# A decoder layer in split fp32: where the split weights lie in memory, relative to the operand they are multiplied with

## The chip, the cores and the metric

The kernel runs on one core of a Trainium2 chip. The metric is device time in microseconds. The kernel before was run three times: median 452.47 us, lowest 451.15, highest 453.2. A further execution was profiled and took 451.82 us.

The core's engines run side by side and are joined by semaphores: TensorE (matrix products; PE in the profile, with PEld for its weight loads), VectorE (DVE), ScalarE (ACT), GpSimd (POOL), and SyncE (SP), which issues most transfers.

## The reference

One layer with two token mixers over one input x of 512 tokens by 1024 channels, fp32 throughout:

```python
h = rms_norm(x, norm_w)
proj = h @ w_in                          # 1024 x 5912: q, k, v, z of mixer A; q, three k/v, gates, z of mixer B; gate_m
o_a = moba_mixer(q_a, k_a, v_a)          # block-sparse attention, 8 heads of 64
k_cmp = rms_norm(compress(kc)); v_cmp = compress(vc)
o_b = nsa_mixer(q_b, k_cmp, v_cmp, ...)  # compressed, selected and window branches
y_a = o_a * silu(z_a);  y_b = o_b * silu(z_b)
g_m = sigmoid(gate_m)                    # 2048 columns
merged = g_m[:, :1024] * (y_a @ w_branch_a) + g_m[:, 1024:] * (y_b @ w_branch_b)
out = x + merged @ w_out
```

With 512 tokens every block and every window is in reach, so both attentions are dense and causal here.

## The kernel before

**Split products.** TensorE multiplies in a reduced fp32 format (fp32r). To keep the precision, the kernel splits each operand into a high part (hi) and the rest (lo) and adds three products, hi·hi, lo·hi and hi·lo (`mm3`, line 374). So a product of one 128-row slice is three matmuls, each with its own load of 128 x 128 stationary weights, and with 256 or 512 columns of the other operand streamed through.

**Weights.** All weights come as tiles of 128 x 512 in one fixed order, the list `tiles`. A `Stream` object (`W`) loads each raw tile by a DMA from SyncE's queue into one of six raw buffers; ScalarE or GpSimd copies it into a hi tile (lines 351 and 355), VectorE or GpSimd subtracts to give the lo tile (line 360). The hi and lo tiles lie in eight pairs of fixed buffers, `whi0` to `whi7` and `wlo0` to `wlo7`, in turn; some tiles of the early projections lie in att buffers instead.

**att.** A pool of 45 buffers of 128 x 512 floats holds nearly everything else: split activations, heads, sums. A new tile takes a free buffer, and waits by semaphore for the last reader of what was there.

**Order.** The order of instructions on each engine is written by a planner that runs while the kernel is built: chains of operations with estimated costs, taken by due time, and four streams (attention, the gemms, the compression, the norm) that share TensorE. The number of buffers of PSUM and of some SBUF tags enters the planner; the att pool does not. Attention and the projections run till about 344 us, with the gate pairs of z and of mixer A mixed in.

**The stages that the change touches.**

- *Compression* (`compress_w`, products in `gemm_chan`, line 677): the projections kc and vc with the weights as stationary operand and 512 columns of the normalized input (`hh`, `hl`) streamed; tile `pgc` in the profile, kc from 51.15 us on, vc between 85 and 96 us. The z projections of mixer A use the same function and name later.
- *Mixer B's gate pairs* (`gate_pair(1, j)`, line 1418, j from 0 to 3): the gate matrix in a Strassen-like scheme of seven products of half size (product numbers 1 to 7), two gate blocks of 128 channels at a time. Each product is four slices of three matmuls, weights stationary, 256 columns streamed (`hh`, `hl` or sums `th`). Tile `pgw`; four pairs from 347.85 us on, with the branch products (`pbr`, 512 columns) between them.
- *The last stage* (`last`, line 1634): merged @ w_out in the same scheme, in the order of products 1, 2, 6, 5, 7, 3, 4. Here the merged activations (`m`, `mh`, `ml`) are stationary and the weights W are streamed, 512 columns for each of two blocks of 128 tokens; of product 4, the second block is done in two halves of 256 columns. Tile `po`, 180 matmuls from 408 us on, then the residual is added on VectorE and stored.

**Where the tiles lie.** A hi or lo buffer is 512 + 32 floats wide, 2176 bytes, which is 8.5 times 256 bytes. hi and lo buffers alternate, so each lo buffer begins 128 bytes off the hi buffer's place modulo 256. `part` (line 604) chooses where in its buffer a tile starts: a tile with a shift begins 16 floats (64 bytes) in, and a lo tile without one begins 32 floats (128 bytes) in, its `side`. `att` buffers (2048 bytes), the input `hh`/`hl` (rows of 2048 bytes) and the other operands all lie at the same remainder modulo 256 as the hi buffers. In this text the distance of a product is the start of its W tile less that of the other operand, modulo 256 bytes: 0 for hi and lo without a shift; 64 (hi) and 192 (lo) with one. With a shift are the tiles under 512 wide (kb, vb) and all gate pairs; without one are kc, vc, the z of mixer A, the branch products and the last stage.

Of the kernel before, what the change touches and what calls it, by code (L numbers as in the profile page):

```python
# [13 lines left out]
F32R = mybir.dt.float32r  # L14
# [7 lines left out]
P = 128  # L22
# [12 lines left out]
POFF = [0, 128, 384, 768]  # L35
WT = 512
SHIFT = 16
NW = 8
AHEAD = 6
SLACK = 3e3  # L40
# [8 lines left out]
XSTEP = 3e3  # L49
XA = 0  # L50
LEAD = 17e3
RAWS = (6, 45)
NRAW, NATT = RAWS
LAND = 1000
SLOW = dict(D=1.01, A=1.01, P=1.05)
# [31 lines left out]
def chan_pieces():  # L87

    out = {"kc": KC, "vc": VC}
    for j in range(4):  # L90
        out[f"za{j}"] = ZA + 128 * j
    return out
# [13 lines left out]
def hybrid_kernel(ctx: ExitStack, tc: tile.TileContext, x, x0, xT, wtok, wchan, wz, wgate, gains, w1,  # L106
                  relone, wbr, wout, consts, out):
    nc = tc.nc
    cp = ctx.enter_context(tc.tile_pool(name="cp", bufs=1))
    wp = ctx.enter_context(tc.tile_pool(name="wp", bufs=NW))  # L110
    pg = ctx.enter_context(tc.tile_pool(name="pg", bufs=2, space=bass.MemoryType.PSUM))
# [9 lines left out]
    def nm(s):  # L121
        uid[0] += 1
        return f"{s}{uid[0]}"
# [304 lines left out]
    def att(name, dt=F32R):  # L428
        return ap_.tile([P, 512], dt, name=nm(name), tag="a")
# [111 lines left out]
    cnames = list(chan_pieces())  # L541

    def tok_tiles(name):
        i0, nt, n, kk = tlay[name]
        return [(wtok[i0 + i][:, :kk * n], kk * n) + (SHIFT,) * (n < WT) for i in range(nt)]

    def chan_tiles(name):
        return [(wchan[cnames.index(name), i], 512) for i in range(2)]

    ORDER_T = ("v", "qk0", "kc", "qk1", "vc", "kb", "qb", "vb", "za0", "za1", "za2", "za3")  # L550
    tiles = []
    for n_ in ORDER_T:
        tiles += tok_tiles(n_) if n_ in tlay else chan_tiles(n_)
    wsum = {w: drp.tile([4, n_, P, 512], F32, name=nm("wsum")) for w, n_ in (("z", 2), (0, 4), (1, 4), (2, 4))}

    def quads(w):

        return wz if w == "z" else wgate[w] if w < 2 else wout

    def operand(p_, w, j):  # L560

        s_ = wsum[w]
        return {1: lambda: quads(w)[0, j], 2: lambda: quads(w)[1, j], 4: lambda: quads(w)[3, j], 5: lambda: s_[0, j], 6: lambda: s_[1, j],
                3: lambda: s_[2, j], 7: lambda: s_[3, j]}[p_]()
# [18 lines left out]
    for q in SEQ:  # L583
        if q in range(8):
            tiles.append((wbr[q, 0], 512))
        else:
            tiles += [(operand(p_, "z" if q[0] == "z" else 0, int(q[1])), 512, SHIFT) for p_ in (1, 2, 6, 5, 7, 3, 4)]
    for j in range(4):
        for p_ in (1, 2):
            tiles.append((operand(p_, 1, j), 512, SHIFT))  # L590
        for p_ in (5, 6, 3, 7):
            tiles.append((operand(p_, 1, j), 512, SHIFT))
        tiles += [(wbr[j, 1], 512), (operand(4, 1, j), 512, SHIFT), (wbr[j + 4, 1], 512)]
    for p_ in (1, 2, 6, 5, 7, 3, 4):
        tiles += [(operand(p_, 2, k), 512) for k in range(4)]
    from_att = set()
    for n_ in ORDER_T:
        if n_ in tlay and tlay[n_][1] == KT:
            o_ = sum(len(tok_tiles(z)) if z in tlay else 2 for z in ORDER_T[:ORDER_T.index(n_)])
            from_att |= set(range(o_, o_ + KT, 2))  # L600
    shift = {i: SHIFT for i in range(len(tiles)) if tiles[i][2:]}
    tiles = [z[:2] for z in tiles]

    def part(name, tag, side):

        place = itertools.count()

        def f(i):
            z = shift.get(i, 0)
            if i in from_att:  # L610
                return att(name)[:, z:]
            b = next(place) % NW
            t = wp.tile([P, WT + 2 * SHIFT], F32R, name=nm(name), tag=f"{tag}{b}", bufs=1)
            return t[:, z or side:]
        return f
    W = Stream(tiles, NRAW - 1, part("wh", "whi", 0), part("wl", "wlo", 2 * SHIFT))
    W1 = W1_[0] = Stream([(w1[kv, q], 512) for kv in range(2) for q in range(8)], 1, lambda i: att("vh"), lambda i: att("vl"))

    def ahead(f):

        W.split(W.i + min(4, int(f * 4 + 0.8)))

    def gemm_tok(name, emit, tags="gggg"):
        _, nt, n, kk = tlay[name]
        ws = []
        for t in range(NT):
            yield room(tags[t])
            ps = psum(tags[t], "pgt")
            for k in range(KT):
                if not t and not k % kk:  # L630
                    ws += W.take(1, n)
                    W.split(W.i + min(nt - 1 - k // kk, 3))
                h = hh[:, k, t * P:(t + 1) * P], hl[:, k, t * P:(t + 1) * P], None
# [8 lines left out]
    def more(n, used):  # L642

        i = W.i
        while i < W.i + n:
            used += i not in from_att
            if used > NW:
                break
            i += 1
        W.split(i)  # L650

# [982 lines left out]
    def last(ms, xr):  # L1634
# [33 lines left out]
        for p_, z_, first in ((1, "a", True), (2, "c", True), (6, "a", False), (5, "b", True), (7, "a", False), (3, "b", False)):  # L1668
            for k in range(4):
                if p_ == 2:  # L1670
                    xr[k, 1] = att("xr", F32)
                    dma(xr[k, 1], x[k * P:(k + 1) * P, 512:], 2048)
                w = W.take(1, 512)[0]
                for t in range(2):
                    if not k:
                        if first:
                            yield room(tags[z_][t])
                            ps[z_, t] = psum(tags[z_][t], "po")
                        else:
                            yield rd[z_, t].ready  # L1680
                    yield from part(ps[z_, t], p_, t, k, w, full, first, not first)
                    if k == 3:
                        rd[z_, t] = add(z_, t, *out_of(p_, t), full)
                        if (p_, t) == (7, 1):
                            add(z_, t, t, 1, False, False, H[1])
        ws = W.take(4, 512)
        for t, z_, z in ((0, "a", full), (1, "a", H[0]), (1, "d", H[1])):
            if z_ == "d":
                yield room("g")
                ps[z_, t] = psum("g", "po")  # L1690
            else:
                yield rd[z_, t].ready
            for k in range(4):
                yield from part(ps[z_, t], 4, t, k, ws[k], z, z_ == "d", z_ == "a")
            add(z_, t, *out_of(4, t), z)
# [122 lines left out]
```

## Time and profile before

| what | us |
|---|---|
| median of 3 runs (lowest, highest) | 452.47 (451.15, 453.2) |
| the profiled execution | 451.82 |
| its span | 450.0 |
| TensorE busy | 442.1 (98%) |
| VectorE busy | 382.5 (85%) |
| ScalarE busy | 302.6 (67%) |
| GpSimd busy | 202.6 (45%) |

A row of a group names line, engine, operation, output<-inputs (of a matmul: the streamed operand, then the stationary one), shape and count. In the chain and in the list of instructions the first two columns are the start and the length in us. A matmul's length runs from its start to the end of its results, and the next one starts long before that; the time that a matmul costs is the distance between two starts. A row of a stretch gives the stretch, the sum, then for each engine its busy time and the number of its instructions that touch the stretch, then the granted clock, the DMA share and GB/s.

### The profile page before, as it was taken

Reading aid. Unit: us, or ns where it says so; the run is one execution under the profiler, and the core shown is the slowest. Engines: PE = TensorE matmul, PEld = TensorE weight load, DVE = VectorE, ACT = ScalarE, POOL = GpSimd, SP = SyncE. Lnnn points to the kernel's source line nnn. Section 1 sums busy time; section 2 is a strip of 40 time slices with the busy share of each in tenths; the row PEclk is TensorE's granted clock in tenths of the full one; section 3 lists DMA queues with packets and bytes.
Section 4 is the critical chain, followed back from the end, with each engine's and each line's share of the span. In section 5 each row is a group of like instructions: output and inputs, shape, how many; then the busy total and the mean of one; then the engine's idle time right before and its main releaser. Section 6 shows DMA issues by size and latency. Waiting matters only on the chain.

```text
span 450.0 us, 8536 instructions
## 1 busy us (share of the span) xinstructions
PE 442.1 (98%) x2779; PEld 394.4 (88%) x2779; DVE 382.5 (85%) x938; ACT 302.6 (67%) x710; POOL 202.6 (45%) x239
## 2 busy tenths in 40 slices
PE   8999999999999999999999999999999999999996
PEld 7888888899778899888999999989988999998885
DVE  5998899889998796879899899977967698899783
ACT  6875778867978798376878777687764355455450
POOL 1364337866675573077675654664850222211000
PEclk9999999999999999999999999999999999999999
DMA  8886646887965869958977876986767888899862
GB/s 263 279 278 212 216 150 207 179 248 182 269 175 168 213 213 282 294 142 189 291 215 212 212 187 175 250 223 156 211 165 171 263 219 253 219 246 313 275 219 95
DMA packets 54221, 98.21 MB, mean 218 GB/s; under 512 B 5216, under 2 KB 8160, under 8 KB 54176
## 3 DMA queue, kind: packets, MB, share of 16 engines
q1 hardware_dynamic: 38944, 68.30, 47.0%
q0 software_dynamic: 7616, 14.68, 20.2%
q10 hardware_dynamic: 7616, 14.68, 9.6%
q8 instruction: 22, 0.36, 0.3%
q14 instruction: 23, 0.19, 0.1%
HBM read 90.69 MB, written 36.31 MB: 282 GB/s over the span
## 4 chain that ended last, share of the span: by engine, by line
PE 82%; DVE 10%; ACT 3%; DMA 2%; issue 2%; SPq 0%; POOL 0%; ACTq 0%; DVEq 0%
PE pgw L385 19%; PE pgt L385 14%; PE pbr L385 10%; PE po L385 9%; PE pgc L385 7%; PE O L1097 6%; PE pt L1063 5%; PE pgf L667 4%; PE sps L1016 3%; PE sps L1017 3%; DMA wr<-in_w 1%; DVE wl L360 1%; DVE sb L1035 1%; DMA wr<-in_wtok 1%; DVE pl L1077 1%
## 5 line engine op out<-in xcount | busy, mean ns | idle before, releaser
L360 DVE TENSOR_TENSOR wl<-wr,wh 128x512 fp32r<-128x512 f32 (+1 forms) x150 | 102.9, 701 | 3.9 <-ACT wh L351 3.6
L351 ACT CAST wh<-wr 128x512 fp32r<-128x512 f32 (+1 forms) x130 | 76.9, 608 | 14.5 <-DMA wr<-wsum 6.1
L355 POOL TENSOR_SCALAR wh<-wr 128x512 fp32r<-128x512 f32 (+1 forms) x39 | 31.0, 807 | 77.7 <-DVE wl L360 21.1
L1054 POOL TENSOR_SCALAR P<-P,sst,gate 128x512 f32<-128x512 f32 (+3 forms) x56 | 46.2, 828 | 39.9 <-DVE sst L1053 31.8
L1050 ACT ACTIVATE P<-sb,sst 128x512 f32<-128x512 f32 (+3 forms) x88 | 50.8, 577 | 17.4 <-DVE sst L1035 15.7
L1035 DVE CUSTOM_DVE_ANT_0 sb<-sps,T 128x512 f32<-128x512 f32 (+3 forms) x96 | 45.9, 482 | 14.0 <-PE sps L1017 13.4
L385 PE MATMUL pgt<-wl,hh 128*128 128x512 f32 (+2 forms) x160 | 55.9, 349 | 0.8 <-DVE wl L360 0.8
L385 PE MATMUL pgt<-wh,hh 128*128 128x512 f32 (+2 forms) x160 | 56.6, 354 | 0.0
L385 PE MATMUL pgt<-wh,hl 128*128 128x512 f32 (+2 forms) x160 | 55.8, 348 | 0.0
L385 PE MATMUL pgw<-th,wh 128*128 128x256 f32 x240 | 48.9, 280 | 0.2 <-DVE gm L1508 0.2
L1075 ACT CAST ph<-pt 128x512 fp32r<-128x512 f32 (+2 forms) x72 | 33.8, 476 | 19.7 <-PE pt L1063 18.2
L385 PE MATMUL pgw<-hh,wh 128*128 128x256 f32 x160 | 45.1, 282 | 0.2 <-ACT c L1449 0.2
L385 PE MATMUL pgw<-hh,wl 128*128 128x256 f32 x160 | 44.4, 277 | 0.0
L385 PE MATMUL pgw<-hl,wh 128*128 128x256 f32 x160 | 44.4, 277 | 0.0
L1063 PE MATMUL pt<-cst,P 128*128 128x128 f32 x232 | 40.7, 273 | 0.4 <-DVE pl L1077 0.3
L1077 DVE TENSOR_TENSOR pl<-pt,ph 128x512 fp32r<-128x512 f32 (+2 forms) x72 | 38.7, 548 | 2.0 <-ACT ph L1075 1.7
L385 PEld LDWEIGHTS pgw<-th,wh 128*128 128x128 f32 x240 | 39.4, 188 | 0.7 <-DVE gm L1508 0.4
L426 POOL TENSOR_TENSOR nr<-nss,mhalf 128x8 f32<-128x8 f32 (+1 forms) x16 | 26.9, 1684 | 20.5 <-DVE nss L425 17.3
L385 PEld LDWEIGHTS pgt<-wl,hh 128*128 128x128 f32 x160 | 30.1, 188 | 5.1 <-DVE wl L360 1.2
L385 PE MATMUL pgw<-th,wl 128*128 128x256 f32 x120 | 33.3, 277 | 0.0
L385 PEld LDWEIGHTS pgt<-wh,hh 128*128 128x128 f32 x160 | 30.1, 188 | 3.4 <-ACT nraw L710 0.2
L385 PEld LDWEIGHTS pgt<-wh,hl 128*128 128x128 f32 x160 | 30.1, 188 | 3.2
(268 smaller groups left out, 1290.7 us busy)
## 6 DMA issues: line engine op xcount, KB each, us to landing
wr<-wsum SPq DMA_DIRECT2D x56, 256.0 KB, 4.3
wr<-in_wtok SPq DMA_DIRECT2D x36, 256.0 KB, 4.8
wsum<-in_wgate ACTq DMA_DIRECT2D x16, 512.0 KB, 5.0
wsum<-wsum POOLq DMA_DIRECT2D x14, 512.0 KB, 8.1
wr<-in_wgate SPq DMA_DIRECT2D x24, 256.0 KB, 5.2
xsum<-th SPq DMA_DIRECT2D x16, 256.0 KB, 2.1
T<-rtab SPq DMA_DIRECT2D x16, 256.0 KB, 5.3
wr<-in_w SPq DMA_DIRECT2D x16, 256.0 KB, 4.6
```

Source lines behind the costliest of these rows:

```text
L351: e.copy(hi, raw)
L355: e.tensor_scalar(hi, raw, 1.0, 1.0, op0=ALU.mult, op1=ALU.mult)
L360: c.do({"D": cd(n)} if lead else either(n), lambda e, hi=hi, lo=lo, raw=raw: e.tensor_sub(lo, raw, hi.bitcast(F32))).mark((w, 1, i))
L385: nc.tensor.matmul(dst, sts[i][a], mvs[i][b], start=(start and i == a == b == 0), stop=(stop and i == n - 1 and b == 1), skip_group_check= ...
L426: c.do({"p": 430 + POWC * w}, lambda e: e.tensor_tensor(v(dst), v(ss), mhalf[:parts, :w], op=ALU.pow))
L1035: e.tensor_tensor_reduce(z["sb"][:, :L], sps[:, :L], T[:, S - L:], scale=-1.0, scalar=3e38, op0=ALU.add, op1=ALU.min, accum_out=st[:, 0, b ...
L1050: e.activation(pv(), z["sb"][:, :L], AF.Exp, bias=st[:, 0, b:b + 1], scale=-1.0, accum_out=st[:, 1, b:b + 1])
L1054: c.do({"P": 315 + 0.834 * L}, lambda e: e.tensor_scalar(pv(), pv(), st[:, 2, b:b + 1], g, op0=ALU.mult, op1=ALU.mult))
L1063: nc.tensor.transpose(pt[:, (b - kb) * P:(b - kb + 1) * P], u.p0 if u.p0 is not None and b == 0 else u.pb[:, POFF[b] + kb * P:POFF[b] + (k ...
L1075: e.copy(z["w"][0], pt[:, :w])
L1077: ch.do({"D": cd(w)}, lambda e: e.tensor_sub(z["w"][1], pt[:, :w], z["w"][0].bitcast(F32)), pt)
L1097: nc.tensor.matmul(O[0][:, S - n:], v.bitcast(F32) if kb == 3 else v, w, start=(u.first and kb == 0 and i == 0), stop=(u.last and kb == 3 ...
```

## The change

Each product gets a shift of its own, in floats, and hi and lo tile get the same. A buffer becomes 512 + 64 floats wide, 2304 bytes or nine times 256, so that hi and lo buffers all begin at the same remainder and `side` goes. The 16 buffers grow by 128 bytes each; the att pool gives up one buffer of 2048 bytes for it.

In bytes, the distances become: last stage, products 1, 2, 6, 5, 7, 3, 4: 16, 32, 48, 64, 96, 240, 224 (all were 0). Mixer B's gate pairs 0 to 3: 32, 16, 96, 240 (were 64 and 192). kc 16, vc 240 (were 0). The other tiles with a shift keep 64 for hi and get 64 for lo in place of 192. The tiles without one keep 0.

```diff
 SHIFT = 16
+SHIFTS = {1: 4, 2: 8, 6: 12, 5: 16, 7: 24, 3: 60, 4: 56, "kc": 4, "vc": 60}
+SHIFT1 = (8, 4, 24, 60)
...
-RAWS = (6, 45)
+RAWS = (6, 44)
...
-        return [(wchan[cnames.index(name), i], 512) for i in range(2)]
+        return [(wchan[cnames.index(name), i], 512, SHIFTS.get(name, 0)) for i in range(2)]
...
         for p_ in (1, 2):
-            tiles.append((operand(p_, 1, j), 512, SHIFT))
+            tiles.append((operand(p_, 1, j), 512, SHIFT1[j]))
         for p_ in (5, 6, 3, 7):
-            tiles.append((operand(p_, 1, j), 512, SHIFT))
-        tiles += [(wbr[j, 1], 512), (operand(4, 1, j), 512, SHIFT), (wbr[j + 4, 1], 512)]
+            tiles.append((operand(p_, 1, j), 512, SHIFT1[j]))
+        tiles += [(wbr[j, 1], 512), (operand(4, 1, j), 512, SHIFT1[j]), (wbr[j + 4, 1], 512)]
     for p_ in (1, 2, 6, 5, 7, 3, 4):
-        tiles += [(operand(p_, 2, k), 512) for k in range(4)]
+        tiles += [(operand(p_, 2, k), 512, SHIFTS[p_]) for k in range(4)]
...
-    shift = {i: SHIFT for i in range(len(tiles)) if tiles[i][2:]}
+    shift = {i: tiles[i][2] for i in range(len(tiles)) if tiles[i][2:]}
...
-    def part(name, tag, side):
+    def part(name, tag):
...
-            t = wp.tile([P, WT + 2 * SHIFT], F32R, name=nm(name), tag=f"{tag}{b}", bufs=1)
-            return t[:, z or side:]
+            t = wp.tile([P, WT + 4 * SHIFT], F32R, name=nm(name), tag=f"{tag}{b}", bufs=1)
+            return t[:, z:]
         return f
-    W = Stream(tiles, NRAW - 1, part("wh", "whi", 0), part("wl", "wlo", 2 * SHIFT))
+    W = Stream(tiles, NRAW - 1, part("wh", "whi"), part("wl", "wlo"))
```

## The prediction, made before the changed kernel was timed

> **What bounds the kernel now.** I read the page's head and its chain first, then the chain in order of time for the last 110 us, then single instructions of TensorE in the three places that the change touches.
>
> ```profile
> span 450.0 us, 8536 instructions
> PE 442.1 (98%) x2779; PEld 394.4 (88%) x2779; DVE 382.5 (85%) x938; ACT 302.6 (67%) x710; POOL 202.6 (45%) x239
> ...
> PE 82%; DVE 10%; ACT 3%; DMA 2%; issue 2%; SPq 0%; POOL 0%; ACTq 0%; DVEq 0%
> ```
>
> TensorE sets the end: 98% busy and 82% of the chain. In the changed stages it is all of the chain (columns: start, length, what, how many):
>
> ```profile
> 348.01 8.17 PE pgw L385 x72
> 356.18 2.74 PE pbr L385 x12
> 358.92 1.37 PE pgw L385 x12
> ...
> 393.09 8.22 PE pgw L385 x72
> ...
> 404.05 1.37 PE pgw L385 x12
> 405.42 2.74 PE pbr L385 x12
> 408.16 38.40 PE po L385 x180
> 446.56 0.02 issue
> 446.59 0.42 DVE xr L1653
> ```
>
> Mixer B's four gate pairs are four groups of 72 and four of 12, 336 matmuls; the last stage is 180. A nanosecond on each of these is a nanosecond on the end. The length that counts is from one start to the next, not the mean of one instruction, since they overlap. So, single instructions (start, length), three in the gate pairs, then the last stage:
>
> ```profile
> 349.21 0.28 PE L385 MATMUL pgw<-hh,wh 128*128 128x256 f32 x1
> ...
> 350.57 0.28 PE L385 MATMUL pgw<-hh,wh 128*128 128x256 f32 x1
> ...
> 351.93 0.28 PE L385 MATMUL pgw<-th,wh 128*128 128x256 f32 x1
> ```
>
> There are 12 matmuls between each two of these rows: 1.36 us / 12 = 113.3 ns for 256 columns, with the weights 64 bytes (hi) and 192 bytes (lo) past the other operand, counted modulo 256.
>
> ```profile
> 411.40 0.39 PE L385 MATMUL po<-wh,mh 128*128 128x512 f32 x1
> ...
> 412.08 0.39 PE L385 MATMUL po<-wh,mh 128*128 128x512 f32 x1
> 412.31 0.39 PE L385 MATMUL po<-wh,ml 128*128 128x512 f32 x1
> 412.53 0.39 PE L385 MATMUL po<-wl,mh 128*128 128x512 f32 x1
> 412.76 0.39 PE L385 MATMUL po<-wh,mh 128*128 128x512 f32 x1
> ...
> 443.87 0.28 PE L385 MATMUL po<-wh,mh 128*128 128x256 f32 x1
> 443.99 0.28 PE L385 MATMUL po<-wh,ml 128*128 128x256 f32 x1
> 444.11 0.28 PE L385 MATMUL po<-wl,mh 128*128 128x256 f32 x1
> 444.23 0.28 PE L385 MATMUL po<-wh,mh 128*128 128x256 f32 x1
> ```
>
> With distance 0 the 512-column matmuls take 0.68 / 3 = 226.7 ns, and the 256-column ones of product 4 take 120 ns, 6.7 ns more than in the gate pairs. That is the one place where this trace shows a distance to matter. TensorE's weight loads show which limit it is:
>
> ```profile
> 443.52:444.95 1.43, 1.43 (x12) 1.00 0.18 66
> 347.85:349.21 1.36, 1.36 (x12) 1.00 0.69 164
> 408.68:415.47 6.79, 6.79 (x31) 5.63 (x30) 6.79 (x14) 3.25 (x7) 1.93 (x2) 1.00 1.05 365
> ```
>
> The first two rows are stretches seen by the weight loads alone: 12 loads in 1.43 us at distance 0, 12 in 1.36 us in a gate pair, back to back in both, so a slower load shows at once. In the third row, of 512-column work (columns: stretch, sum, PE, weight loads, then the other engines), loads fill only 5.63 of 6.79 us: a load that gets some nanoseconds slower or faster there is hidden by the streaming of 512 columns. And 226.7 is exactly twice 113.3: streaming costs 0.4427 ns per column in both, with distance 0 in the one and 64/192 in the other. I take that rate as a floor that the distance does not touch. The clock column is 1.00, so the clock is no part of it.
>
> **The change part by part.** It adds and removes no instruction, and the order is the same: the planner's costs are untouched, and it does not count the att tiles. What moves is addresses, and one att buffer goes.
>
> *Last stage, 156 matmuls of 512 columns* (products 1, 2, 6, 5, 7, 3 with 24 each, and 12 of product 4). Distance goes from 0 to 16, 32, 48, 64, 96, 240 and 224 bytes. By the floor above: 0. Bounds: no row has such a distance. Below, the best that a row has shown a distance to do is 6.7 ns a matmul, −1.04 us; above, distance 0 is already the slow row among those seen, so I bound it by the same step the other way, +1.04. I take 0, because loads have 1.16 us of slack in the 6.79 us row.
>
> *Last stage, 24 matmuls of 256 columns* (product 4, distance 0 to 224, that is 32 bytes to the other side). Ends 113.3 and 120 ns: −0.16 to 0. Half way between 0 and 64, I take half: −0.08 us.
>
> *Gate pairs, 4 × 84 matmuls of 256 columns.* Distance goes from 64/192 to 32, 16, 96, 240 for pairs 0 to 3. They stand on the floor now and have no slack in the loads, so there is more to lose than to win. Upper end, all as at distance 0: 336 × 6.7 = +2.24 us. Lower end, a load alone:
>
> ```profile
> 158.36 0.60 PE L1063 MATMUL pt<-cst,P 128*128 128x128 f32 x4
> ...
> L1063 PE MATMUL pt<-cst,P 128*128 128x128 f32 x232 | 40.7, 273 | 0.4 <-DVE pl L1077 0.3
> ```
>
> Four transposes span 0.60 us and the last lasts 0.273, so they start (0.60 − 0.273) / 3 = 109 ns apart; with only 128 columns to stream, that is the load's own pace. 336 × (113.3 − 109) = −1.44 us if floor and collision both went. I go by the nearest rows, in a straight line from 120 ns at 0 to 113.3 at 64 bytes on either side: 16 bytes (pairs 1 and 3) costs 5 ns, 32 bytes (pair 0) 3.3 ns, 96 bytes (pair 2) nothing. 84 × (3.3 + 5 + 0 + 5) = +1.12 us.
>
> A rule speaks against any of this. The Trainium skill, "TensorE: Matmul & The Clock Gate", section "Step-by-step: what each phase is for", gives TensorE two independent read ports, one for the moving operand and one for weight loads. By it the two could not collide, distance would be nothing and the whole sum 0; the 120 against 113.3 ns above does not agree with it, and I go with the rows.
>
> *Compression, 48 matmuls of 512 columns* (kc to 16 bytes, vc to 240).
>
> ```profile
> 51.15:56.59 5.44, 5.44 (x24) 4.32 (x23) 0.00 (x0) 1.00 0.69 230
> 85.44:95.59 10.15, 6.37 (x24) 4.17 (x24) 0.00 (x0) 1.00 0.84 189
> ...
> 93.38 5.96 DMA wr<-in_w
> ```
>
> kc is 24 matmuls in 5.44 us, 226.7 ns each, on the floor with loads at 4.32 of 5.44: 0, bounds ±0.16 by 6.7 ns each. vc is spread over 10.15 us among attention's work, and a weight transfer stands on the chain behind it (the chain's row at 93.38): 0, hidden by that transfer; ±0.16 if that cover went.
>
> *The lo tiles of the other shifted products* move from 192 to 64 bytes, where the hi tiles already are. Here, in the vb projection, W is the moving operand:
>
> ```profile
> 173.13 0.28 PE L385 MATMUL pgt<-wl,hh 128*128 128x256 f32 x1
> ...
> 174.31 0.28 PE L385 MATMUL pgt<-wh,hh 128*128 128x256 f32 x1
> ```
>
> Ten matmuls in 1.18 us, 118 ns; at worst 120, so 96 × 2 and the same for kb: 0 to +0.4 us; I take +0.1. The six gate pairs of z and mixer A have 168 lo matmuls (a third of 504), bounded by 6.7 ns each, 0 to +1.1; I take 0, as twice as many hi loads at 64 bytes go along with 113.3 ns.
>
> *44 att buffers instead of 45.* A writer of an att tile can wait for a reader that ends later. The densest place I found is VectorE's pair of y tiles ahead of the branch products:
>
> ```profile
> 312.49 0.68 DVE L1126 TENSOR_TENSOR ys<-O,ot 64x512 f32<-64x512 f32 x1
> 313.20 1.49 DVE L1145 TENSOR_TENSOR yl<-ys,yh 128x512 fp32r<-128x512 f32 x2
> 314.61 0.15 DVE L1053 RECIPROCAL sst<-sst 128x1 f32<-128x1 f32 x1
> ```
>
> A wait there holds up what is queued behind it on VectorE: the reciprocal of attention's softmax, which GpSimd and then TensorE's transposes need, and the next read of a score bank. Ends 0 and 1.49 us (the pair's own length again); I take +0.1, as TensorE has matmuls of other streams (branch products, gate pairs) queued between attention's and fills in with them; without that cover it is the 1.49.
>
> *The splits that write the tiles* write at another start, with the same count and shape; 0, hidden behind TensorE, whose gate pairs need nothing from VectorE on the chain.
>
> Sum: 0 − 0.08 + 1.12 + 0 + 0.1 + 0 + 0.1 = +1.24 us. The profiled execution took 451.82 us (450.0 of span and 1.8 around it), which gives 453.1. The runs' median is 452.47, 0.65 above that execution, inside a spread of 451.15 to 453.2; the straight line that carries the +1.12 is the weakest step, so I do not add the whole 0.65 on top: **453.0 us**.
>
> **The rivals.**
>
> *A, the distance frees the 512s too* (faster). The rate of 0.4427 ns a column would then be a collision that all distances in multiples of 64 bytes share. For it: every such distance in the trace is a multiple of 64 bytes. Against it: the cost grows with the columns streamed, not with the loads. Priced by the lower ends: −1.04 − 0.16 − 1.44 − 0.16 = −2.8 us, 449.0. A sentence beside it: the same page of the Trainium skill, section "Back-to-back issue gap", gives columns / 2.4 + 2.5 ns, an estimate of 215.8 ns for 512 and 109.2 for 256; by that all three stages would lose 156 × 10.9 + 24 × 10.8 + 336 × 4.1 + 24 × 10.9 = 3.6 us, 448.2. The rows here, 226.7 and 113.3, do not show it.
>
> *B, near distances collide harder* (slower). One mechanism, in the gate pairs: the load that runs beside 256 columns meets them in the same place of memory, and a distance of one or two 16-byte steps keeps the two together longer than distance 0. It is slower by over 0.5% once the four pairs average over 120 ns, where +2.24 is reached; at twice distance 0's loss, 126.7 ns, it is +4.5, 456.3. For it: loads have no slack there, 1.36 of 1.36 us. Against it: no row is above 120 in a quiet stretch.
>
> *C, the distance does nothing,* and 120 against 113.3 comes from which operand is the weights: product 4 loads m and streams W, the gate pairs the other way round. For it: the vb projection, W streamed too, takes 118 ns at 64 and 192 bytes. Then the sum is +0.2, 452.0 to 452.7.
>
> *D, the att buffer* bites: 1.49 us at its place and as much at one more, +3 us, 454.8. For it: VectorE's next attention step stands right behind the pair in the rows at 313 us, so nothing of a wait there is private. Against it: VectorE is 85% busy, not 98%, and can catch up. It decides from about 2.3 us of waits that reach TensorE.
>
> **How the numbers follow.** Forecast (between −1 and +2.2 us, 451.2 to 454.5) 0.55, C 0.20, A 0.11, B 0.09, D 0.05. About 0.5%, 2.3 us, is what a measurement of this kernel can tell from no change. Faster is A without its weak half and a little of the forecast's low side: 0.11. Slower is B, most of D and the top of the forecast: 0.14. The rest, 0.75, is within. The range takes half of A and of B: 450.0 to 455.2.
>
> **What would show it.** In the gate pairs, 12 matmuls should take 1.42 us in pairs 1 and 3 (118.3 ns each), 1.40 in pair 0 (116.6), 1.36 in pair 2. In the last stage 512 columns stay at 226.7 in every product, and product 4's halves fall to about 117 ns; 113.3 would mean that 32 bytes do as much as 64. If any product of the last stage is under 224 ns, A is right and the floor was none. If all gate pairs keep 1.36 us and the halves 120, C is right. If the gate pairs pass 1.44 us, B. A wait on an att tile would show as an idle stretch of VectorE around 313 us, with one of TensorE behind it. The forecast is wrong if the gate pairs together change by over 2.3 us.

## The result

The change makes the kernel slower: 455.42 us, median of 7 runs (454.43 to 456.03), against 452.31 us for 7 runs of the kernel before beside it. The ratio is 1.0071, with a 95% interval of 1.0056 to 1.0086: +3.2 us (2.5 to 3.9). The forecast was 453.0 us and "within 0.5%"; its range ended at 455.2. The profiled execution took 455.2 us, of which 453.4 are span, 3.4 more than before.

### The profile page after: what moved, and what is told of

It is laid out like the page before. It is cut to its first block, busy times and chain, and to the rows that moved or that the text cites. A ratio compares the mean times of both kernels' runs of the same rounds, so it can differ in the third digit from the quotient of the medians.

```text
span 453.4 us, 8542 instructions
## 1 busy us (share of the span) xinstructions
PE 444.6 (98%) x2779; PEld 396.2 (87%) x2779; DVE 382.6 (84%) x938; ACT 302.7 (67%) x710; POOL 201.6 (44%) x239
## 4 chain that ended last, share of the span: by engine, by line
PE 82%; DVE 11%; ACT 3%; issue 2%; DMA 2%; SPq 0%; DVEq 0%; ACTq 0%
PE pgw L387 18%; PE pgt L387 14%; PE pbr L387 9%; PE po L387 9%; PE pgc L387 7%; PE O L1099 6%; PE pgf L669 5%; PE pt L1065 5%; PE sps L1018 3%; PE sps L1019 3%; DVE wl L362 2%; DMA wr<-in_wbr 1%; DVE sb L1037 1%; DVE pl L1079 1%; DVE vl L362 1%
## 5 line engine op out<-in xcount | busy, mean ns | idle before, releaser
L1065 PEld LDWEIGHTS pt<-cst,P 128*128 128x128 f32 x232 | 29.1, 140 | 5.3 <-issue 1.5
```

The lines of the kernel that those rows point to most:

```text
L1065: nc.tensor.transpose(pt[:, (b - kb) * P:(b - kb + 1) * P], u.p0 if u.p0 is not None and b == 0 else u.pb[:, POFF[b] + kb * P:POFF[b] + (k ...
```

## The profile after

The head of the page and the engines' shares of the chain:

```profile
span 453.4 us, 8542 instructions
PE 444.6 (98%) x2779; PEld 396.2 (87%) x2779; DVE 382.6 (84%) x938; ACT 302.7 (67%) x710; POOL 201.6 (44%) x239
...
PE 82%; DVE 11%; ACT 3%; issue 2%; DMA 2%; SPq 0%; DVEq 0%; ACTq 0%
```

TensorE executes the same 2779 matmuls in the same order and is busy 2.5 us longer. The page counts 8542 instructions, 6 more than before; the difference is in semaphore instructions alone, and the kernel that changes nothing but the att buffers has it too. The chain in order of time from the gate pairs on (start, length, what, how many; helper lines are two further down than before):

```profile
348.82 8.52 PE pgw L387 x72
357.34 2.78 PE pbr L387 x12
360.12 1.42 PE pgw L387 x12
...
379.75 8.45 PE pgw L387 x72
388.20 2.74 PE pbr L387 x12
...
393.89 6.01 DMA wr<-in_wbr
...
400.07 0.40 ACT mh L1360
400.47 0.28 ACT c L1451
...
400.88 3.05 PE pgw L387 x24
403.94 2.76 PE pbr L387 x12
406.70 1.41 PE pgw L387 x12
...
410.86 39.07 PE po L387 x180
```

Against the rows of before, the 3.4 us fall into three stretches. The gate pairs begin at 348.82 in place of 348.01: +0.81. They and the branch products up to the last stage take 410.86 − 348.82 = 62.04 us in place of 408.16 − 348.01 = 60.15: +1.89. The last stage takes 39.07 in place of 38.40: +0.67. In the middle stretch, 72 gate matmuls take 8.52 (pairs 0 and 1) and 8.45 (pair 2) in place of 8.17, and 12 take 1.42 or 1.41 in place of 1.37; counted from start to start over all 336, the gate products account for +1.45. Most of the rest, about 0.4, is a stall in pair 3: its 72 matmuls take 8.87 us from start to start, and not 8.45 as in pair 2, because two groups of twelve took 1.76 and 1.49 us. There TensorE waited for ScalarE's c, which on the chain stands behind a transfer of branch weights.

The first stretch holds a wait of VectorE that before did not have (columns: start, length, instruction, and in brackets the idle time ahead of it and what ended that):

```profile
312.28 0.68 DVE L1128 TENSOR_TENSOR ys<-O,ot 64x512 f32<-64x512 f32 x1
314.09 1.49 DVE L1147 TENSOR_TENSOR yl<-ys,yh 128x512 fp32r<-128x512 f32 x2 [1.13 <-PE sps L1019]
315.50 0.15 DVE L1055 RECIPROCAL sst<-sst 128x1 f32<-128x1 f32 x1
```

It is the y pair that the prediction named. The row puts its wait down to a matmul of the scores, which has to read what lay in the att tile, and the reciprocal behind it goes from 314.61 to 315.50. TensorE then waits behind VectorE, which is late with its split of attention's transposed tile (first the row of before, then that of after; columns: who waited for whom, us in total, times, the longest):

```profile
PE pt L1063 <- DVE pl L1077: 0.3, 1, 0.3
PE pt L1065 <- DVE pl L1079: 1.4, 1, 1.4
```

The execution had been 0.21 us ahead of that of before at 311 us, so that stretch's +0.81 is +1.03 from there on, less 0.21.

## The experiments

**44 att buffers alone** (kernel before):

```diff
-RAWS = (6, 45)
+RAWS = (6, 44)
```

> The kernel before with 44 att buffers in place of 45 and nothing else; all distances stay. Theory T (the trace of after shows VectorE's yl pair 1.1 us late at 314 us, behind a matmul of the scores): the missing buffer alone costs 1.0 to 1.2 us, so the time is 1.1 us above before (ratio 1.0025), the pair starts near 314 us, and the gate pairs (12 in 1.36 us) and the last stage (38.4 us) are untouched. Rival: the wait is hidden and the 1.1 us at 315 us came with the distances; then the ratio is 1.000 and the pair starts near 313.2 us.

12 runs: 453.21 us against 452.70, ratio 1.0011 (1.0000 to 1.0021), that is +0.5 us (0 to 0.95). VectorE's row and, from the chain, the changed stages:

```profile
314.98 1.49 DVE L1145 TENSOR_TENSOR yl<-ys,yh 128x512 fp32r<-128x512 f32 x2 [1.14 <-PE sps L1017]
```

```profile
349.79 8.17 PE pgw L385 x72
360.70 1.37 PE pgw L385 x12
...
409.98 38.44 PE po L385 x180
```

The wait is the buffer's, with the distances left as they were. All the later kernels bear this out. From the mixer-A gate product that starts at about 311 us to mixer B's first gate product, the four kernels profiled with 45 buffers take 36.87 to 36.89 us, and the eight with 44 take 37.89 to 38.00: +1.0 to 1.1 us each time. Of the twelve executions, one of each kernel, eleven reach the first of these points between 310.7 and 311.6 us, and one (the next experiment's) at 313.0; the timed runs of the kernel before alone spread over 2 us. So a profiled span says nothing below 2 us, while a stretch of it does. The timed +0.5 lies below the expected 1.1 and has its upper end just below this 1.0; whether part of the wait is recovered on average, the runs do not settle.

**The same distances at other places** (kernel before): an unused tile of 32 bytes ahead of all others, so that every tile lies 32 bytes further on.

```diff
+    pad = cp.tile([P, 8], F32, name="pad")
...
+    nc.gpsimd.memset(pad, 0.0)
```

> The kernel before with 32 unused bytes per partition ahead of everything, so that every tile lies 32 bytes further and all distances stay. Theory T, distance: gate pairs 12 matmuls in 1.36 us, last stage 226.7 ns for 512 columns and 120 ns for 256, as before. Rival, the place itself (a start that is no multiple of 64 bytes from where it was): the last stage goes to 230 to 235 ns for 512 columns and the gate pairs to 117 to 118 ns, as with 32 bytes in the changed kernel.

One execution: 454.18 us. From its chain:

```profile
350.06 8.17 PE pgw L385 x72
...
410.52 38.39 PE po L385 x180
```

Gate pairs and last stage are as before. So for a move of 32 bytes, the only one tried, it is the distance between the operands that counts and not where they lie. (Its span is longer through the stretch before 311 us and a stall of 0.3 us in gate pair 3.)

**Many distances in one kernel** (layout of after): another multiple of 16 bytes, or of 4, for each gate product, branch tile and last-stage tile, hi and lo alike (kb, vb, kc and vc move as well; not shown).

```diff
+    G1 = [4 * (n % 16) for n in range(16)] + [1, 2, 3, 6, 14, 18, 30, 34, 46, 50, 58, 62]
+    L1 = [4 * n for n in range(16)] + [1, 2, 6, 14, 18, 46, 58, 62] + [16, 32, 48, 8]
...
-            tiles.append((operand(p_, 1, j), 512, SHIFT))
+            tiles.append((operand(p_, 1, j), 512, G1[next(gi)]))
...
-        tiles += [(operand(p_, 2, k), 512) for k in range(4)]
+        tiles += [(operand(p_, 2, k), 512, L1[next(li)]) for k in range(4)]
...
```

> The changed kernel with another distance for each product or tile: mixer B's gate pairs run through all sixteen steps of 16 bytes and twelve places between the steps, the 24 tiles of the last stage's first six products the same, the branch products, kb, vb, kc and vc some more. A map. Theory T (the weight load that runs beside a stream collides with it by distance modulo 256): 256 columns with W as weights 113.3 ns at 64 bytes and only in a band about it, up to 120 elsewhere; 512 columns 226.7 at 0 and 228 to 237 elsewhere, nothing under 224; the map differs between W as weights and W as the stream by the sign of the distance. Rival, lines of 16 bytes: all multiples of 16 alike and only the places between them differ. Rival, a floor that gives way: some place with 512 columns under 220 ns.

One execution: 455.45 us. From start to start, the last stage in ns per matmul and the gates in us for twelve (distance in bytes, W counted from the other operand):

```
gates, 256 columns   0: 1.431  16: 1.419  32: 1.420  48: 1.411  64: 1.376  80: 1.429  96: 1.407
                   128: 1.419 160: 1.433 192: 1.411 208: 1.400 224: 1.414 240: 1.407
last stage, 512      0: 226.7  16: 230-233  32: 233  48: 231-234  64: 233  80: 231-232  96: 233
                   128: 230-235 160: 233-236 192: 231-232 208: 233-235 224: 232 240: 229.3, then 226.7
```

The places between the steps of 16 bytes are no better (1.40 to 1.44 us, and 230 to 238 ns), nor are 112, 144 and 176 (1.42 to 1.44, and 231 to 233). No 512-column product is below 226.7 ns, so rival A is dead as far as these distances go: that is the floor. But 0 already stands on it, and nearly every other distance leaves it by 4 to 8 ns on a tile's average. For 256 columns one distance stands out, 64, and the straight line from 0 to 64 bytes does not exist: 16, 32, 48, 80 and 96 are all at 1.41 to 1.43, as far as 0 is. Branch products of 512 columns took 2.76 to 2.81 us for twelve at the eight distances tried, against 2.75 at 0.

**64 bytes again, but for hi and lo alike** (layout of after, the rest at 0):

```diff
-SHIFTS = {1: 4, 2: 8, 6: 12, 5: 16, 7: 24, 3: 60, 4: 56, "kc": 4, "vc": 60}
-SHIFT1 = (8, 4, 24, 60)
+SHIFTS = {1: 0, 2: 0, 6: 0, 5: 0, 7: 0, 3: 0, 4: 0, "kc": 0, "vc": 0}
+SHIFT1 = (16, 16, 16, 16)
```

> The changed kernel's layout (576 wide, 44 att buffers) with gate pairs at 64 bytes for hi and lo, and the last stage and the compression at 0. Theory T: what the distances cost comes back, what the buffer costs stays: 1.1 us above before, gate pairs 12 in 1.36 us, last stage 38.3 us. Rival (hi and lo must lie at different distances, 64 and 192, as before): the gate pairs stay at 1.40 us or more and the time at about 2.5 us above before. Rival (the wider buffers themselves cost): gate pairs and last stage as in the changed kernel.

7 runs: 454.72 us, ratio 1.0033 (1.0013 to 1.0054). From its chain:

```profile
349.51 8.48 PE pgw L387 x72
360.73 1.42 PE pgw L387 x12
...
411.79 38.42 PE po L387 x180
```

The last stage is back at 38.4 with distance 0. The gate pairs are not back: all take 1.413 us for twelve, 117.8 ns each, although hi lies at 64 bytes as it did before. What is missing is that lo lay at 192. The time, +1.5 us (0.6 to 2.4), lies between the 1.1 and the 2.5 that were expected and does not tell them apart.

**hi at 64, lo at 192** (the same, but with a pair of shifts for each tile; `part` is told again which of the two it makes):

```diff
-SHIFT1 = (16, 16, 16, 16)
+SHIFT1 = ((16, 48),) * 4
...
             z = shift.get(i, 0)
+            z = z[side] if isinstance(z, tuple) else z
...
```

> The kernel after with 0 for the last stage and the compression, and with mixer B's gate pairs at 64 bytes for the hi tile and 192 bytes for the lo tile (what the kernel before has, but in the wider tiles and with 44 attention buffers). If hi and lo must lie at different distances, twelve products take 1.36 us again, the gate stretch is 8.17/1.37 us on the chain of waits, and the kernel lies at the time of the one with 44 buffers alone: 0.1% above before (0 to 0.3%), span near 451.9 us. If the wider tiles themselves, or what runs ahead of these products, set the pace, twelve take 1.41 us as with 64/64, and the span is near 453.3 us, 0.3% above before. The last stage takes 38.4 us either way.

8 runs: 454.48 us (452.26 to 457.01), ratio 1.0039 (1.0016 to 1.0061). From its chain:

```profile
349.31 8.17 PE pgw L387 x72
360.22 1.37 PE pgw L387 x12
...
400.36 3.02 PE pgw L387 x24
...
410.24 38.39 PE po L387 x180
```

The gates take 8.17 and 1.37 again, in the wide tiles and with 44 buffers: the lost pace was in the lo tile's distance as much as in hi's. The time is above what was expected, 0 to 0.3%. The profiled execution, of 453.9 us, has a stall in gate pair 3, as in after but 0.8 us long: twelve of its matmuls took 2.05 us and the next twelve 1.50, between two groups at 1.36. Whether the other executions have it is not known.

**The last stage's and the compression's distances on top of that:**

```diff
-SHIFTS = {1: 0, 2: 0, 6: 0, 5: 0, 7: 0, 3: 0, 4: 0, "kc": 0, "vc": 0}
+SHIFTS = {1: 4, 2: 8, 6: 12, 5: 16, 7: 24, 3: 60, 4: 56, "kc": 4, "vc": 60}
```

> The same, but with the last stage's and the compression's distances as in the kernel after. If the parts add up, the last stage takes 39.07 us on the chain in place of 38.4, and the kernel is 0.7 us above the one with 64/192 and 0 run beside it (0.15%), the gates being what they are there. If the last stage's loss came from what ran ahead of it, it takes 38.4 us.

7 runs: 454.38 us, ratio 1.0041 (1.0027 to 1.0055). From its chain:

```profile
349.03 8.17 PE pgw L387 x72
...
409.13 39.26 PE po L387 x180
```

The last stage loses 0.87 us through its own distances, with the gates ahead of it at full pace. That is 0.19 more than the same distances lose in after: product 5, at 64 bytes in both, takes 233 ns a matmul here and 229 there, so a distance has no single price here either. The expected 0.7 between the two kernels does not show in the times: the medians differ by −0.1 us, with intervals of about 1.0 and 0.6 us to either side. The stall that the other kernel's execution has is absent here. This kernel differs from after in the gate pairs' distances alone, and lies 0.0030 below it in ratio, 1.4 us, near what the gate products' starts gave (+1.45). The two ratios were measured at different times, each against its own runs of the kernel before, and their intervals together leave about 0.9 us to either side, so the agreement is closer than the times can show.

**Pairs of distances** (the same layout, another pair hi/lo for each gate product and last-stage tile):

```diff
+    gi, li = iter([(16, 48), (48, 16), (16, 16), (0, 32), ...]), iter([(0, 0), (0, 32), (32, 0), ...])
...
-            tiles.append((operand(p_, 1, j), 512, SHIFT1[j]))
+            tiles.append((operand(p_, 1, j), 512, next(gi)))
...
-        tiles += [(operand(p_, 2, k), 512, SHIFTS[p_]) for k in range(4)]
+        tiles += [(operand(p_, 2, k), 512, next(li)) for k in range(4)]
```

> Layout of the kernel after with another pair of distances (hi, lo) for each product of mixer B's gate pairs and for each tile of the last stage. Theory: what counts is that hi and lo differ by 128 bytes: 64/192, 192/64, 32/160, 0/128, 96/224 and 16/144 give 1.36 to 1.38 us for twelve of 256 columns, and 64/64, 192/192, 64/96, 64/128, 64/0 and 0/64 give 1.40 to 1.43. Rival one: only 64 and 192 are good, whatever the other (32/160, 0/128, 96/224 and 16/144 give 1.40 to 1.43). Rival two: what ran before decides, and the same pair gives both values at different places. In the last stage (512 columns) only a tile with both at 0 takes 226.7 ns each; if hi and lo apart by 128 were enough there too, 0/128, 128/0, 64/192 and 32/160 would give it as well; if each operand counts for itself, 0/128 lies between 226.7 and 233 ns.

One execution: 454.79 us. Ten of the gate products, seen by their weight loads, which are back to back there (columns: stretch, its length, busy time and count of the loads, clock, DMA share, GB/s; 13 where a neighbour's load reaches in):

```profile
349.17:350.54 1.37, 1.36 (x12) 1.00 0.48 180
351.90:353.26 1.36, 1.36 (x13) 1.00 0.80 303
353.26:354.69 1.43, 1.43 (x13) 1.00 0.87 254
354.69:356.11 1.42, 1.42 (x13) 1.00 1.05 181
...
364.45:365.86 1.41, 1.41 (x12) 1.00 0.61 149
365.86:367.25 1.39, 1.39 (x13) 1.00 0.79 118
...
375.62:377.06 1.44, 1.44 (x12) 1.00 0.58 172
382.65:384.03 1.38, 1.38 (x13) 1.00 1.04 387
384.03:385.39 1.36, 1.36 (x13) 1.00 0.99 377
385.39:386.81 1.42, 1.42 (x13) 1.00 0.64 192
```

In order (hi/lo, in bytes) they are 64/192, 64/64, 0/128, 32/160; 64/64 behind a branch product, 64/192; 128/0, 64/192, 64/64, 0/64. Being 128 bytes apart is not enough: 0/128, 32/160 and 128/0 are slow, and so were 96/224 and 16/144. So the theory falls and rival one, "only 64 and 192 are good", is nearest. But the second rival holds as well: 64/64 takes 1.36 us behind a fast product, twice, and 1.41 behind a branch product. In the last stage, three matmuls at a time, a tile with 0/128 took 229 to 231 ns each and 64/192 228 to 235; 0/0 took 226.7 at the start of the stage, and at two later places, behind slower tiles, first 230 to 231 and then 226.7. So 0/128 lies between, as if each operand counted for itself, and here too what ran ahead plays a part.

**What runs ahead** (layout and rest as there; pair 0: 64/192 once, then 64/64 six times; pair 1: 64/64 twice, 64/192, 64/64 three times, 64/192; pair 3: 16/16, 64/64 twice, 64/192, 64/64, 16/16, 64/64; the last of each behind a branch product):

```diff
+    gi = iter([(16, 48), (16, 16), (16, 16), (16, 16), (16, 16), (16, 16), (16, 16), ...])
...
```

> Mixer B's gate pairs again, the last stage and the compression at 0, 44 buffers. Theory from the pairs of distances: 64/192 takes the products into a fast pace (113.3 ns for 256 columns, 1.36 us for twelve), and 64/64 and 192/192 keep that pace once it is there but do not reach it. Pair 0: first product 64/192, the next five 64/64, the one behind the branch product 64/64: 1.37, then five times 1.36, and 1.41 for the last. Pair 1: 64/64 twice, 64/192, 64/64 three times, 64/192 behind the branch product: 1.41 twice, 1.36 to 1.39, 1.36 three times, 1.37. Pair 2: 64/192, then 64/64, 192/192, 64/64, 192/192, 64/64, and 64/192 behind the branch product: 1.37 and 1.36 throughout. Pair 3: 16/16, then 64/64 twice, 64/192, 64/64, 16/16, and 64/64: 1.42, 1.41 twice, 1.36 to 1.39, 1.36, 1.42, 1.41. Rival: each product's own distances decide, and every 64/64 takes 1.41 whatever ran ahead, as in the kernel with 64/64 throughout.

One execution: 454.33 us. From its chain:

```profile
348.95 8.17 PE pgw L387 x72
357.12 2.74 PE pbr L387 x12
359.87 1.42 PE pgw L387 x12
...
364.03 8.30 PE pgw L387 x72
...
378.03 7.96 DMA wr<-in_wbr
...
395.50 8.28 PE pgw L387 x72
...
406.51 1.42 PE pgw L387 x12
```

Pair 0's 72 matmuls, 60 of them at 64/64, take 8.17 us, against 8.48 where all lay at 64/64. The row behind the branch product, 64/64 too, takes 1.42. In pair 1 the two ahead of the 64/192 take 1.414 and 1.413, that one 1.387, and the three behind it 1.36 each. So the same instruction with the same distances has two paces, and what ran ahead decides which. One point missed: in pair 3, 64/64 behind a 16/16 product took 1.363 and not 1.41. It reaches the fast pace from some slow products and from none of the branch products at distance 0 that ran directly ahead of it. Pair 2 cannot be read: it held the stall, 1.2 to 1.3 us here.

**The gates alone, with 45 buffers** (kernel before, hi 32 and lo 160):

```diff
-            tiles.append((operand(p_, 1, j), 512, SHIFT))
+            tiles.append((operand(p_, 1, j), 512, SHIFT // 2))
...
```

> The kernel before (45 attention buffers, tiles 544 wide, the rest at its own distances) with mixer B's gate pairs alone at 32 bytes for hi and 160 for lo in place of 64 and 192. From the map of pairs, twelve products of 256 columns take 1.415 to 1.425 us in place of 1.36: 28 times 0.055 to 0.065 us, the kernel 1.5 to 1.8 us above before (ratio 1.0033 to 1.0040), the gate stretch 8.50/1.42 us on the chain of waits, and no VectorE wait at 314 us beyond that of before. If instead the fast pace hangs on something else in this layout, nothing changes.

12 runs: 453.84 us against 452.54, ratio 1.0028 (1.0017 to 1.0038), +1.3 us (0.8 to 1.7). From its chain, and VectorE's y pair:

```profile
348.62 8.56 PE pgw L385 x72
...
375.43 1.43 PE pgw L385 x12
...
410.59 38.40 PE po L385 x180
```

```profile
313.81 1.49 DVE L1145 TENSOR_TENSOR yl<-ys,yh 128x512 fp32r<-128x512 f32 x2
```

The gate products take 1.43 us for twelve, 1.8 us more in all from start to start; the timed 1.3 lies below the expected 1.5 to 1.8, whose lower part its interval still takes in. VectorE's pair does not wait.
**The last stage alone, with 45 buffers** (kernel before, 64/192):

```diff
-        tiles += [(operand(p_, 2, k), 512) for k in range(4)]
+        tiles += [(operand(p_, 2, k), 512, SHIFT) for k in range(4)]
...
```

> The kernel before with the last stage's tiles alone at 64 bytes for hi and 192 for lo in place of 0. From the map of pairs, 512 columns take 228 to 235 ns in place of 226.7 (mean 231.4: 156 times 4.7 ns, 0.74 us) and 256 columns about 113.5 in place of 120 (24 times 6.5 ns, 0.16 us off): the last stage 38.9 to 39.1 us on the chain in place of 38.4, the kernel 0.5 to 0.7 us above before (ratio 1.0012 to 1.0015). By the rule that a different distance is good at any width, it is 0.16 us below before.

12 runs: 452.90 us against 452.54, ratio 1.0010 (0.9999 to 1.0022), +0.5 us (−0.05 to 1.0). From its chain:

```profile
348.22 8.17 PE pgw L385 x72
...
408.64 38.78 PE po L385 x180
```

The stage was expected at 38.9 to 39.1 us. The 512-column matmuls took 230.5 ns on average (231.4 expected), and the 24 of 256 columns about 117 and not the expected 113.5; at 64/192, but behind 512-column products.

Both parts lengthen the chain by themselves, without the buffer's wait and without each other: the pair that gives 256 columns their best pace costs the last stage 0.4 us on the chain. In the times, the gates' loss is clear; the interval of the last stage's reaches no change. No setting in these runs beats what the kernel before has, so no faster version came out of them.

## Why the prediction was wrong

By its own sum the change should have added 1.24 us; the span shows 3.4. Two steps failed: the last stage's distances, put at nothing, and the att buffer's wait, put at a tenth of what it cost; together they are 1.6 of the 2.2 us that were missed. Term by term:

- **Last stage, 512 columns: predicted 0, measured about +0.7** (39.07 against 38.40 in after, 39.26 against 38.39 with the gates undisturbed). This step is the one that was wrong in kind. It read 0.4427 ns a column as a floor "that the distance does not touch" and hid any slower load behind 1.16 us of slack in the load row. The floor is real, but distance 0 was what kept the products on it. The products get slower, by 2 to 10 ns in 226.7 and by 5.6 on average, 0.87 us in all, and load slack does not cover that. About 0.16 of it does not show, because in the seven kernels at distance 0 one matmul of product 2 takes 0.11 us longer, behind VectorE's split of its lo tile, and its neighbours some ns; the five slower kernels have no such matmul. Its upper bound of +1.04 held.
- **Product 4's 256 columns: predicted 120 to 117 ns; measured 118** (24 × 2 = −0.05 us against −0.08). Right.
- **Gate pairs: predicted +1.12, measured +1.45.** The place and the sign were right. The straight line was not: pair 2 at 96 bytes was to stay at 1.36 us and took 1.41, pair 0 took 1.42 and not 1.40, pair 1 1.42 as predicted, pair 3 1.41 and not 1.42. Any of the four leaves the fast pace, by 4 to 5 ns a matmul, and how far it moves hardly counts. The loss stayed within the bound of 2.24. That the total came this near is in part luck, since the line that it was read from does not exist.
- **44 att buffers: predicted +0.1, measured +1.0 in the trace** (0 to 0.95 timed). The tile, the engine, the queue behind it and the bounds were right. The cover that the sum relied on was not there: TensorE waits 1.4 us behind VectorE at that place in place of 0.3, and does not fill in with other streams. The sum took the low end of its bounds against its own row, which showed the reciprocal right behind the pair.
- **lo tiles of the other products: predicted +0.1; measured nothing that stands out.** The execution was 0.2 us ahead of that of before at 311 us, which is little beside the spread of the runs. z's and mixer A's gate products, quoted at 0, average 115.0 ns with 64/64 and 115.3 with 64/192.
- **Compression: predicted 0, and kc took the same 5.44 us for 24 matmuls** at 16 bytes. Right. vc, in groups among attention's work, averaged 229 ns a matmul at 240 bytes, against 232 at 0 in the kernel before.
- **No instruction added:** TensorE's order is the same, but the missing buffer adds six semaphore instructions.
- **Not foreseen: the stall in gate pair 3**, about 0.4 us.

Of the rivals, A (faster) is dead, since nothing fell below 226.7 and 113.3 ns. C is dead, since both stages moved with the distance alone. B, that near distances collide harder than 0, was right that there is only loss to be had in the gates, but none of after's pairs passed its 1.44 us. D, the att buffer, happened once and at its named place, 1.1 us and not 1.49; no second place shows. The change as it was thus came out as the forecast's mechanism, plus a part of D, plus a loss in the last stage that no case had.

The prediction weighed a rule of the Trainium skill, page "TensorE: Matmul & The Clock Gate", section "Step-by-step: what each phase is for", of two independent read ports, and went with the rows. The single-edit kernels do not agree with what the prediction drew from that rule either: 8.56 in place of 8.17 us for the gates, and 38.78 in place of 38.40 for the last stage, by addresses alone.

The parts add up in the trace (1.0 + 1.45 + 0.7 + 0.4 − 0.2 = 3.35 of 3.4). What stays open is how often the stall happens. It was plain in four of the eight executions with 44 buffers and, at 0.3 us, in two of the four with 45; in three of the four the chain passes a transfer of branch weights ahead of it, of 6.0 (after), 6.5 (64/64 throughout) and 8.0 us (64/64 behind 64/192), but in the fourth (64/192) it passes VectorE's work instead, and the kernel before has transfers of these weights of up to 7.0 us and a stall of under 0.1. So its cause stays open, and so does whether the change makes it likelier.

## What to carry to other kernels

A stage that stands on its floor can only lose by having its operands moved, so ask first which stages are on it and whether the present addresses are what put them there; slack in the weight loads says nothing about the streams. Two points of a map (120 at 0, 113.3 at 64/192) are no ground for a straight line: here the good values were isolated, and a pair of addresses was good where either alone was not. And when a pool gives up a buffer, price the wait at the densest place at its full length unless a row shows the engine behind it filling in.

## What the runs showed of the hardware

The time of these matmuls depends on where their operands lie relative to each other, counted modulo 256 bytes; moving all by 32 bytes changed nothing. The values are 113.3 or 117 to 120 ns for 256 columns, 226.7 or 228 to 238 for 512, at a granted clock of 1.00. In an unbroken run, 512 columns are good at distance 0, and 256 columns at 64 with 192. In short groups among other work that does not hold: vc, three to nine 512-column matmuls at a time, averaged 230 to 232 ns in the nine kernels that have it at distance 0, and 229 in the two that have it at 240 bytes.

There are two paces for one and the same product. With 64/64, 256 columns take 113.3 ns behind products that were at that pace, and 117.8 behind a branch product, for twelve matmuls and for 72, until something else brings them over; 64/192 reached the fast pace by itself in nearly every case (one 192/64 product behind a branch product stayed at 118.8, and the 24 products of the last stage with W streamed took about 117). With 512 columns it is similar on one side: weights 16 bytes past the streamed operand kept 226.7 ns over all 24 matmuls of kc, which follow a projection at that pace, and product 3 of after's last stage, which lies the same way, took 231 to 238 behind slow ones. The other way round, with the streamed operand 16 bytes past the weights, 230 to 233 followed directly on 226.7. What in the memory makes these paces was not tried.
